# One ordering edge and the order of the last two column blocks in a two-layer encoder

## The chip, the cores and the metric

The kernel runs on one core of one Trainium2 chip. The metric is the device time of one execution in microseconds (us). The kernel before takes 2002.78 us (median of three runs, 2001.56 to 2003.46).

A core has five engines, each with its own queue of instructions that it works off in order. TensorE (PE) multiplies; its weight loads (PEld) overlap the multiplications. VectorE (DVE), ScalarE (ACT) and GpSimd (POOL) do element-wise work, and SyncE (SP) issues DMA transfers. Engines wait for each other by semaphores.

## The reference

The reference is a trunk of two encoder layers over 256 tokens of width 2048, in float32. Each layer has attention (layer 0: neighbourhood attention; layer 1: grouped-query attention; both beside four cross-attention heads into 256 memory tokens), an output projection, and an MLP. What concerns this change is the MLP and the end:

```python
n = rms_norm(h, mlp_norm[i])
h = h + jnp.square(jax.nn.relu(n @ w_up[i])) @ w_down[i]
...
return rms_norm(h, final_norm)
```

`w_up` is 2048 x 8192 and `w_down` 8192 x 2048. The final norm divides each token's row by its root mean square and multiplies by `final_norm` column by column.

## The kernel before

The 256 tokens lie in two token tiles of 128 partitions (`NT` = 2). Every float32 matrix product is made of three products of rounded numbers: each operand is split into a high part (a copy on ScalarE, L507) and a low part (the original minus the high part, on VectorE, L508), and TensorE adds high x high, high x low and low x high. So every weight that comes from HBM passes through ScalarE and VectorE before TensorE can use it.

**The up projection** makes 128 hidden columns at a time (`up_grains`, number m of 64), as two grains of eight k-steps each. After it, `squared` applies ReLU and square; when m is odd, the two columns m-1 and m make a *pair* (number m // 2), for which VectorE forms sums and differences of its four 128x128 blocks (L1122 to L1124) and splits them into `a_s` (L1126). That split is what `box["made"]` remembers.

**The down projection** takes 30 of the 32 pairs for each half of the output columns by a Strassen scheme with seven products in place of eight (`down_grains`, step n of 60; `STEPS` gives the half q and the pair j of each step; steps 0 and 1 are pairs 0 and 1 of half 1, step 2 is pair 0 of half 0). One step loads a 1 MB chunk `b` of four 128x512 blocks and needs besides three running sums of them:

- `lift`: ScalarE copies block 3 into `t` (L1165), and an accumulating DMA of GpSimd adds block 1 to it (L1166).
- `pre`: VectorE forms the three other sums of `t`, one on top of the other (L1172 to L1174).
- `prep_first` splits `b` into `bh`, `bl`; `prep_second` splits `t` into `th`, `tl`. These four rooms exist once each.
- `run`: TensorE's first half has three products (nine matmuls with `bh`, `bl`), its second half four (twelve matmuls with `th`, `tl`; L1195, L1198, L1199).

The grains of a layer's MLP stand in a list: four up projections, and then for each step the first half of the down step, the two grains of an up projection, and the second half. While grain k runs, loads, sums and splits of grains some places ahead are traced; `pre` is traced five grains ahead, the splits four.

**Order on an engine.** The order in which the instructions of one engine stand in its queue is worked out by a planner when the program is built: it simulates the program in time and takes what is ready, earlier-traced work first. The kernel adds edges: `tc.issue_after(x)` says that the instructions in its block stand behind instruction x in the queue of x's engine. No semaphore is added by it. In `pre`, steps 1 and 2 have such an edge behind the split that `box["made"]` holds at that moment; it is the split of the latest pair traced by then. `pin` keeps marked instructions in the order in which the program lists them.

**The end.** The two pairs that are left over are summed plainly, by column blocks of 512 in the order 2, 0, 1, 3 (`REST`; `plain_grains`). A block has two pieces of weights, of two k-steps each; both token tiles are summed together, piece by piece, in `m_products` (L388, L391, L392). Then `down_done` adds the sums to `h` (L1241), takes the squares on ScalarE (L920), and for layer 1 multiplies by `final_norm` (L1358). In layer 1 the last block (3) is different: it is summed tile by tile, tile 0 in one part of 512 columns and tile 1 in two parts of 256, and each part goes to `finish`. It adds to `h` (L1409), forms the mean of squares over all four blocks, takes its power -1/2 on GpSimd (L1432), multiplies the tile's row (L1433 to L1435 on VectorE and ScalarE), and issues three DMA transfers to the output (L1438).

Of the kernel before, what the change touches and what calls it, by code (L numbers as in the profile page):

```python
# [14 lines left out]
ALU = mybir.AluOpType  # L15
# [144 lines left out]
def encoder_kernel(ctx: ExitStack, tc: tile.TileContext, t: dict, out: bass.AP):  # L160
# [945 lines left out]
    def squared(layer, m, ps):  # L1106

        e = m % 2
        if e == 0:
            box["c"] = at.mlp.tile([P, 8, P], F32, tag="c", bufs=2, name="c")  # L1110
        c = box["c"]
        two = c[:, 2 * e : 2 * e + 2, :].rearrange("p a b -> p (a b)")
        box["relu"] = nc.scalar.activation(two, ps, AF.Relu)
        nc.scalar.activation(two, two, AF.Square)
        if e == 0:
            return
        pair = m // 2
        if pair >= max(STEPPED):
            a = at.mlp.tile([P, 2, 4, P], F32R, tag="a", bufs=6, name="a_p")
            split(a[:, 0], a[:, 1], c[:, :4])  # L1120
        else:
            nc.vector.tensor_tensor(c[:, 4, :], c[:, 0, :], c[:, 2, :], op=ALU.subtract)  # L1122
            nc.vector.tensor_tensor(c[:, 5:7, :], c[:, 0:8:4, :], c[:, None, 1, :].to_broadcast([P, 2, P]), op=ALU.add)
            nc.vector.tensor_tensor(c[:, 7, :], c[:, 3, :], c[:, 6, :], op=ALU.subtract)  # L1124
            a = at.mlp.tile([P, 2, 7, P], F32R, tag="a", bufs=6, name="a_s")
            box["made"] = split(a[:, 0], a[:, 1], c[:, 1:])[1]  # L1126
            if pair >= min(STEPPED):

                n = pair - min(STEPPED)
                if n == 0:  # L1130
                    box["a_0"] = at.mlp.tile([P, max(STEPPED) - min(STEPPED), 2, P], F32R, tag="a", bufs=6, name="a_0")
                split(box["a_0"][:, n, 0], box["a_0"][:, n, 1], c[:, 0])
        box["a", pair] = a
        if m == UPS - 1 and layer == 1:
            later(2, load_gf)
# [11 lines left out]
    def down_grains(layer, n, begins, ends, sooner):  # L1147

        q, j = STEPS[n]
        own = {}  # L1150

        def load():
            own["b"] = at.side.tile([P, 4, 512], F32, tag="b", bufs=3, name="b")
            nc.sync.dma_start(own["b"].rearrange("p a b -> p (a b)"),
                              t[f"w_pair{layer}"][j * 2 + q])

        def behind(fn, far=4):

            return (lambda: past(fn, box["splits"][-far])) if n < 2 else fn

        def lift():

            b, s = own["b"], at.side.tile([P, 4, 512], F32, tag="T", bufs=2, name="t")
            own["t"] = s
            nc.scalar.activation(s[:, 3, :], b[:, 3, :], AF.Copy)  # L1165
            nc.gpsimd.dma_start(s[:, 3, :], b[:, 1, :], accum_op=ALU.add)  # L1166

        def pre():

            b, s = own["b"], own["t"]  # L1170
            with tc.issue_after(box["made"].ins) if n in (1, 2) else nullcontext():
                nc.vector.tensor_tensor(s[:, 0, :], b[:, 3, :], b[:, 0, :], op=ALU.add)  # L1172
            nc.vector.tensor_tensor(s[:, 1, :], s[:, 0, :], b[:, 1, :], op=ALU.add)
            nc.vector.tensor_tensor(s[:, 2, :], s[:, 1, :], b[:, 2, :], op=ALU.add)  # L1174

        def prep_first():
            own["first"] = tuple(at.mlp.tile([P, 3 * 512], F32R, tag=x, name=x) for x in ("bh", "bl"))
            split(*own["first"], own["b"].rearrange("p a b -> p (a b)")[:, : 3 * 512])

        def prep_second():  # L1180
            own["second"] = tuple(at.mlp.tile([P, CH], F32R, tag=x, name=x) for x in ("th", "tl"))
            with tc.issue_after(box["relu"].ins) if n == 0 else nullcontext():
                split(*own["second"], own["t"].rearrange("p a b -> p (a b)"))

        def run(which, products):
            if n == 0 and which == "first":
                open_strassen(layer)
            hi, lo = own.pop(which)
            a = box["a", j]
            for name, ai, bi in products:  # L1190
                if n == 0:
                    sum_of(name)
                entered = begins and not (name in SHARED and q in box["z_set"])
                ps, s = box["ps"][name], slice(bi * 512, (bi + 1) * 512)
                ins = nc.tensor.matmul(ps, a[:, 0, ai, :], hi[:, s], start=entered, stop=False,  # L1195
                                       skip_group_check=True)
                pin(ins)
                nc.tensor.matmul(ps, a[:, 0, ai, :], lo[:, s], start=False, stop=False, skip_group_check=True)  # L1198
                nc.tensor.matmul(ps, a[:, 1, ai, :], hi[:, s], start=False, stop=ends, skip_group_check=True)  # L1199

        def after(products):
            if ends:
                for name, _, _ in products:
                    taken(q, name)
                    if n + 1 < len(STEPS):
                        seeded(STEPS[n + 1][0], name)

        def after_second():
            after(SECOND)
            if ends:  # L1210
                box["z_set"].add(q)
            if ends and j == STEPPED[q] - 1:
                folded(q, 0.5 if n == len(STEPS) - 1 else 1)

        return [Grain(lambda: run("first", FIRST), lambda: after(FIRST), load, behind(pre), behind(prep_first, 4 if n else 1),
                      (8 if n < 2 else 12, 8 if sooner else 5, 4), behind(lift)),
                Grain(lambda: run("second", SECOND), after_second, None, None, behind(prep_second), SOONER)]
# [62 lines left out]
    def plain_grains(layer, nb, at_chunk):  # L1280

        last = layer == 1 and nb == REST[-1]
        w = Work("M", None, left_of, 0, True, True, None, finish if last else down_done(layer, nb))
        nc_ = len(chunks_left(nb))
        own = {}

        def load(c):
            own[c] = loaded(t[f"w_plain{layer}"][at_chunk + c], "Ub"[(at_chunk + c) % 2])

        def prep(c, hf):  # L1290
            if (at_chunk + c) % 2 == 0:
                own[c, hf] = half_of_side(own[c], hf, MOVING_AT)
            else:
                own[c, hf] = tuple(at.mlp.tile([P, HALF], F32R, tag="bt"[hf] + x, name=f"{x}_p") for x in "hl")
                box["rest"] = split(*own[c, hf], own[c][:, hf * HALF : (hf + 1) * HALF])


        PIECES = [(c, hf, ((UPS // 2 - min(STEPPED)) // 2 - nc_ + c) * 4 + hf * 2, 2) for c in range(nc_) for hf in range(2)]

        def begin():  # L1300
            if nb == REST[0]:
                closed("ps_sums")
                open_sums(layer)
            w.ps = [at.acc.tile([P, 512], F32, tag="acc", name="ps_m") for _ in range(NT)]
            if last:

                w.ps.append(at.acc.tile([P, 512], F32, tag="acc", name="ps_m"))

        def run(n):
            if last:  # L1310
                return
            c, hf, k0, nk = PIECES[n]
            if n == 0:
                begin()
            for i in range(NT):
                m_products(w, k0, nk, i, *own[c, hf], n == 0, n == len(PIECES) - 1)

        def after():
            if not last:
                w.done(w)  # L1320
                return

            begin()

            for i, bank, part in ((0, 0, (0, 512)), (1, 1, (0, 256)), (1, 2, (256, 512))):
                for n, (c, hf, k0, nk) in enumerate(PIECES):
                    m_products(w, k0, nk, i, *own[c, hf], n == 0, n == len(PIECES) - 1, keep_order=True, part=part,
                               bank=bank)
                w.done(w, i, bank, *part)

        return [Grain(lambda n=n: run(n), after if n == len(PIECES) - 1 else None,
                      (lambda c=c: load(c)) if hf == 0 else None, None, lambda c=c, hf=hf: prep(c, hf), SOON)
                for n, (c, hf, _, _) in enumerate(PIECES)]
# [21 lines left out]
    def times_gf(nb):  # L1355
        s = slice(nb * 512, (nb + 1) * 512)
        for i in range(NT):
            nc.vector.tensor_tensor(h[:, i, s], h[:, i, s], box["gf"][:, s], op=ALU.mult)  # L1358

    def down_done(layer, nb):  # L1360
        def f(w):
# [419 lines left out]
```

## Time and profile before

| | before |
|---|---|
| time, median of three runs | 2002.78 us |
| profiled execution: time | 2002.76 us |
| profiled execution: span, first to last instruction | 2001.0 us |
| mean granted TensorE clock | 0.997 of full |
| TensorE busy | 1984.8 us, 99% |
| VectorE busy | 1726.2 us, 86% |
| ScalarE busy | 1443.1 us, 72% |
| HBM read | 397.78 MB |

All starts of instructions are counted from the start of the span. A row of a timeline has the start, the duration, the engine, the line of the program, the operation with its output and inputs by the program's names, the shape, and how many were merged into the row (x2); in brackets stands how long the engine had been idle and which instruction released it. Row durations of one engine overlap a little at their ends, so the next start says more of the pace than the sum of durations. `c`, `t`, `b`, `th`, `tl`, `bh`, `bl`, `uh`, `ul`, `a_s` are the rooms named above (`uh`, `ul` are the split weights of the up projection); `first` in the rows of the end is the tile that holds `h`.

### The profile page before, as it was taken

What the parts mean: (1) busy time and instruction counts of PE and PEld (TensorE: products, weight loads), DVE (VectorE), ACT (ScalarE), POOL (GpSimd) and SP (SyncE); (2) the same over time, 40 slices, a digit from 0 to 9 for tenths busy, and PEclk for the clock granted to TensorE, in tenths of its full rate; (3) what the DMA queues carried; (4) which work ended last, traced back from release to release, by engine and by line L of the source; (5) the groups of instructions that cost most, each with busy time, mean ns of one, the idle gap of its engine ahead of it and who ended that gap; (6) DMA issues with size and microseconds to landing.
All of it is one profiled execution on the core that took longest, in us unless ns stands there. A gap on an engine that the chain in (4) does not pass through costs nothing.

```text
span 2001.0 us, 33096 instructions
## 1 busy us (share of the span) xinstructions
PE 1984.8 (99%) x12832; PEld 1801.8 (90%) x12832; DVE 1726.2 (86%) x2096; ACT 1443.1 (72%) x2105; POOL 149.9 (7%) x205
## 2 busy tenths in 40 slices
PE   9999999999999999999999999999999999999998
PEld 9999999898999999999998888898999999999997
DVE  6777767579999999999999869778999999999997
ACT  6655555577887788877887666667788777877786
POOL 0000000000000000000001011000000000000001
PEclk9999999999999999999999999999999999999999
DMA  7855555667777777777778765667777777777775
GB/s 288 320 193 204 206 192 185 261 211 217 223 228 237 234 235 235 221 241 226 229 227 229 263 216 174 225 202 229 226 226 230 237 231 231 237 226 243 228 225 152
DMA packets 110685, 452.46 MB, mean 226 GB/s; under 512 B 18880, under 2 KB 40640, under 8 KB 63168
## 3 DMA queue, kind: packets, MB, share of 16 engines
q1 hardware_dynamic: 90144, 413.38, 60.3%
q0 software_dynamic: 20096, 36.45, 10.4%
q8 instruction: 100, 1.64, 0.3%
q14 instruction: 57, 0.47, 0.1%
q10 hardware_dynamic: 288, 0.52, 0.1%
HBM read 397.78 MB, written 4.19 MB: 201 GB/s over the span
## 4 chain that ended last, share of the span: by engine, by line
PE 98%; DVE 1%; ACT 1%; issue 0%; POOL 0%; DVEq 0%; POOLq 0%
PE ps_u L411 35%; PE p L1198 10%; PE p L1199 10%; PE p L1195 10%; PE ps_s L411 9%; PE ps_m L391 8%; PE ps_m L392 8%; PE ps_m L388 7%; PE sc_ps L604 0%; PE sc_ps L605 0%; PE sc_ps L603 0%; PE av L696 0%; PE av L697 0%; PE av L698 0%; PE idle L240 0%
## 5 line engine op out<-in xcount | busy, mean ns | idle before, releaser
L411 PE MATMUL ps_u<-hT,uh 128*128 128x256 f32 x3874 | 674.5, 276 | 0.0
L411 PEld LDWEIGHTS ps_u<-hT,uh 128*128 128x128 f32 x3874 | 588.5, 188 | 5.8
L411 PE MATMUL ps_u<-hT,ul 128*128 128x256 f32 x1994 | 550.7, 276 | 0.0
L507 ACT ACTIVATE uh<-raw_U 128x1024 fp32r<-128x1024 f32 x262 | 277.5, 1060 | 154.3 <-PE ps_u L411 149.8
L411 PEld LDWEIGHTS ps_u<-hT,ul 128*128 128x128 f32 x1994 | 374.3, 188 | 0.0
L507 ACT ACTIVATE hi<-raw 128x1024 fp32r<-128x1024 f32 (+1 forms) x215 | 222.0, 1037 | 183.0 <-PE ps_m L392 94.2
L508 DVE TENSOR_TENSOR lo<-raw,hi 128x1024 fp32r<-128x1024 f32 (+1 forms) x215 | 255.0, 1190 | 108.4 <-ACT hi L507 107.7
L508 DVE TENSOR_TENSOR ul<-raw_U,uh 128x1024 fp32r<-128x1024 f32 x262 | 319.6, 1220 | 15.7 <-ACT uh L507 15.7
L508 DVE TENSOR_TENSOR tl<-t,th 128x2048 fp32r<-128x2048 f32 x120 | 274.7, 2290 | 57.5 <-ACT th L507 57.3
L507 ACT ACTIVATE th<-t 128x2048 fp32r<-128x2048 f32 x120 | 230.8, 1924 | 90.4 <-PE p L1199 90.4
L508 DVE TENSOR_TENSOR bl<-b,bh 128x1536 fp32r<-128x1536 f32 x120 | 210.3, 1752 | 0.3 <-ACT bh L507 0.3
L1198 PE MATMUL p<-tl,a_s 128*128 128x512 f32 x480 | 188.9, 394 | 5.7 <-DVE tl L508 5.7
L1166 POOL DMA_DIRECT2D t<-b x120 | 104.2, 869 | 1169.4 <-ACT t L1165 1113.2
L1195 PE MATMUL p<-th,a_s 128*128 128x512 f32 x480 | 188.8, 393 | 0.2
L1199 PE MATMUL p<-th,a_s 128*128 128x512 f32 x480 | 188.0, 392 | 0.0
L507 ACT ACTIVATE bh<-b 128x1536 fp32r<-128x1536 f32 x120 | 178.6, 1488 | 3.7
L411 PE MATMUL ps_s<-nT,hi 128*128 128x256 f32 x896 | 154.6, 277 | 0.0
L1199 PE MATMUL p<-bh,a_s 128*128 128x512 f32 x360 | 140.9, 391 | 0.0
L1198 PE MATMUL p<-bl,a_s 128*128 128x512 f32 x360 | 140.1, 389 | 0.0
L1195 PE MATMUL p<-bh,a_s 128*128 128x512 f32 x360 | 140.1, 389 | 0.0
L411 PEld LDWEIGHTS ps_s<-nT,hi 128*128 128x128 f32 x896 | 135.3, 188 | 0.2
L411 PE MATMUL ps_s<-nT,lo 128*128 128x256 f32 x448 | 124.2, 277 | 0.0
(292 smaller groups left out, 3639.9 us busy)
## 6 DMA issues: line engine op xcount, KB each, us to landing
raw_U<-in_w_up SPq DMA_DIRECT2D x128, 1024.0 KB, 6.3
b<-in_w_pair SPq DMA_DIRECT2D x120, 1024.0 KB, 5.8
raw<-in_w_o SPq DMA_DIRECT2D x32, 1024.0 KB, 5.0
t<-b POOLq DMA_DIRECT2D x120, 256.0 KB, 6.5
raw<-in_w_b SPq DMA_DIRECT2D x21, 1024.0 KB, 5.7
raw<-in_w_av SPq DMA_DIRECT2D x12, 1024.0 KB, 5.0
raw<-in_w_aq SPq DMA_DIRECT2D x12, 1024.0 KB, 5.0
raw<-in_w_ak SPq DMA_DIRECT2D x12, 1024.0 KB, 4.9
```

The costliest lines, as they stand in the source:

```text
L388: first = nc.tensor.matmul(ps, ah, hi[:, s], start=st, stop=False)
L391: nc.tensor.matmul(ps, ah, lo[:, s], start=False, stop=False)
L392: final = nc.tensor.matmul(ps, al, hi[:, s], start=False, stop=sp)
L411: ins = nc.tensor.matmul(ps, x, acts[:, k, part], start=k == n == 0, stop=k == KT - 1 and n == 2)
L507: first = nc.scalar.activation(dst_hi, src, AF.Copy)
L508: return first, nc.vector.tensor_tensor(dst_lo, src, dst_hi.bitcast(F32), op=ALU.subtract)
L1166: nc.gpsimd.dma_start(s[:, 3, :], b[:, 1, :], accum_op=ALU.add)
L1195: ins = nc.tensor.matmul(ps, a[:, 0, ai, :], hi[:, s], start=entered, stop=False, skip_group_check=True)
L1198: nc.tensor.matmul(ps, a[:, 0, ai, :], lo[:, s], start=False, stop=False, skip_group_check=True)
L1199: nc.tensor.matmul(ps, a[:, 1, ai, :], hi[:, s], start=False, stop=ends, skip_group_check=True)
```

## The change

The split of a pair is remembered under the pair's number, and the sums of step n (n = 1 or 2) stand behind the split of pair n - 1, where both stood behind the latest split traced. This is done in both layers.

In layer 1 the last two column blocks, 1 and 3, are interleaved by token tile: block 1's grains sum token tile 0 alone, and what is done with the result is done for that tile; then block 3's tile 0 is summed and finished; then block 1's tile 1 is summed with its own additions, squares and multiplication; then block 3's tile 1 follows in its two parts as before.

```diff
-            box["made"] = split(a[:, 0], a[:, 1], c[:, 1:])[1]
+            box["made", pair] = split(a[:, 0], a[:, 1], c[:, 1:])[1]
...
-            with tc.issue_after(box["made"].ins) if n in (1, 2) else nullcontext():
+            with tc.issue_after(box["made", n - 1].ins) if n in (1, 2) else nullcontext():
                 nc.vector.tensor_tensor(s[:, 0, :], b[:, 3, :], b[:, 0, :], op=ALU.add)
...
+        parted = layer == 1 and nb == REST[-2]
...
-            for i in range(NT):
+            for i in range(1 if parted else NT):
                 m_products(w, k0, nk, i, *own[c, hf], n == 0, n == len(PIECES) - 1)
 
+        def second():
+            for n, (c, hf, k0, nk) in enumerate(PIECES):
+                m_products(w, k0, nk, 1, *own[c, hf], n == 0, n == len(PIECES) - 1, keep_order=True)
+            tile_done(w, nb, 1)
+
         def after():
+            if parted:
+                tile_done(w, nb, 0)
+                box["second"] = second
+                return
...
             for i, bank, part in ((0, 0, (0, 512)), (1, 1, (0, 256)), (1, 2, (256, 512))):
+                if bank == 1:
+                    box["second"]()
                 for n, (c, hf, k0, nk) in enumerate(PIECES):
...
+    def tile_done(w, nb, i):
+        s = slice(nb * 512, (nb + 1) * 512)
+        add_scaled(h[:, i, s], w.ps[i], box["inv"][:, i : i + 1])
+        sum_squares(3, i, nb)
+        nc.vector.tensor_tensor(h[:, i, s], h[:, i, s], box["gf"][:, s], op=ALU.mult)
```

## The prediction

> **What bounds the kernel now.** I read the page first, then TensorE's own waits.
>
> ```profile
> span 2001.0 us, 33096 instructions
> PE 1984.8 (99%) x12832; PEld 1801.8 (90%) x12832; DVE 1726.2 (86%) x2096; ACT 1443.1 (72%) x2105; POOL 149.9 (7%) x205
> PE p L1198 <- DVE tl L508: 5.7, 2, 2.8
> ```
>
> The reader is to see that TensorE is the bound: time can come only from its idle time, from matmuls at a lower clock, or from what follows its last matmul. The third line (the waits of TensorE) says that apart from the kernel's first microsecond it waited twice, 5.7 us together, both times for a VectorE instruction that writes `tl`, the low part of a step's sums. The timeline of TensorE puts one in each layer, in the second half of step 1 of the stepped down projection (layer 0, then an undisturbed step 2, then layer 1; start, duration):
>
> ```profile
> 460.48 0.50 PE L1195 MATMUL p<-th,a_s 128*128 128x512 f32 x1
> 463.82 0.50 PE L1198 MATMUL p<-tl,a_s 128*128 128x512 f32 x1 [2.84 <-DVE tl L508]
> 468.02 0.39 PE L1195 MATMUL p<-bh,a_s 128*128 128x512 f32 x1
> 475.52 0.40 PE L1195 MATMUL p<-th,a_s 128*128 128x512 f32 x1
> 478.25 0.39 PE L1195 MATMUL p<-bh,a_s 128*128 128x512 f32 x1
> 1369.01 0.50 PE L1195 MATMUL p<-th,a_s 128*128 128x512 f32 x1
> 1372.35 0.76 PE L1198 MATMUL p<-tl,a_s 128*128 128x512 f32 x1 [2.84 <-DVE tl L508]
> 1376.58 0.39 PE L1195 MATMUL p<-bh,a_s 128*128 128x512 f32 x1
> ```
>
> The twelve matmuls of such a half take 478.25 - 475.52 = 2.73 us in step 2, but 468.02 - 460.48 = 7.54 us in step 1 of layer 0 and 1376.58 - 1369.01 = 7.57 us in layer 1. So a stall costs 4.81 and 4.84 us, not its 2.84 us of idle time. The rest, about 1.97 us, is clock. Busy time by stretches (stretch, length, TensorE busy, granted clock, DMA share, GB/s):
>
> ```profile
> 464.50:467.50 3.00, 3.00 (x9) 0.50 0.60 131
> 1372.30:1375.70 3.40, 3.35 (x8) 0.52 0.72 198
> ```
>
> After each stall some 3.4 us of matmuls ran at half clock.
>
> Why `tl` is late stands in VectorE's timeline of layer 0 (rows in between are left out; the last one is of layer 1):
>
> ```profile
> 440.38 1.09 DVE L508 TENSOR_TENSOR a_s<-c,a_s 128x896 fp32r<-128x896 f32 x1 [1.02 <-ACT a_s L507]
> 443.39 1.23 DVE L508 TENSOR_TENSOR ul<-raw_U,uh 128x1024 fp32r<-128x1024 f32 x1 [0.79 <-ACT uh L507]
> 445.47 2.29 DVE L508 TENSOR_TENSOR tl<-t,th 128x2048 fp32r<-128x2048 f32 x1 [0.85 <-ACT th L507]
> 451.49 1.07 DVE L508 TENSOR_TENSOR a_s<-c,a_s 128x896 fp32r<-128x896 f32 x1
> 452.48 1.29 DVE L1172 TENSOR_TENSOR t<-b 128x512 f32<-128x512 f32 x2
> 457.48 1.28 DVE L1174 TENSOR_TENSOR t<-t,b 128x512 f32<-128x512 f32 x2
> 458.68 1.75 DVE L508 TENSOR_TENSOR bl<-b,bh 128x1536 fp32r<-128x1536 f32 x1
> 461.49 2.28 DVE L508 TENSOR_TENSOR tl<-t,th 128x2048 fp32r<-128x2048 f32 x1
> 470.66 2.29 DVE L508 TENSOR_TENSOR tl<-t,th 128x2048 fp32r<-128x2048 f32 x1 [1.55 <-ACT th L507]
> ...
> 1361.00 1.29 DVE L1172 TENSOR_TENSOR t<-b 128x512 f32<-128x512 f32 x2
> ```
>
> The first sum (L1172) of step 1 and of step 2 come as a pair, x2, directly behind pair 1's split (`a_s` at 451.49): both wait for the same split. The sums are not done before 458, and `tl` starts at 461.49, when TensorE already wants it. VectorE has no gap in this time (a stretch; busy time of TensorE, its loads, VectorE third with 5.00 of 5.00, ScalarE, GpSimd):
>
> ```profile
> 455.00:460.00 5.00, 5.00 (x47) 5.00 (x46) 5.00 (x8) 4.08 (x4) 0.00 (x0) 1.00 0.78 241
> ```
>
> Layer 1 has the same picture 908.5 us later.
>
> **Part one: the edge of step 1.** When step 1's sums are traced, the latest pair that was split is pair 1; when step 2's are traced it still is pair 1. So the new key changes step 1 alone, from pair 1 to pair 0; step 2 keeps its wait. No instruction is added or removed. Three sums of about 0.64 us each (half of the 1.29 us of 452.48), 1.9 us in all, may now stand behind pair 0's split, from 441.4 on. Their data are there, by ScalarE's timeline:
>
> ```profile
> 437.30 0.63 ACT L1165 ACTIVATE t<-b 128x512 f32<-128x512 f32 x1 [0.70 <-DMA b<-in_w_pair]
> 454.27 0.60 ACT L1250 ACTIVATE z<-p 128x512 f32<-128x512 f32 x1 [1.32 <-PE p L1199]
> 458.53 1.90 ACT L507 ACTIVATE th<-t 128x2048 fp32r<-128x2048 f32 x1
> ```
>
> Step 1's chunk `b` had landed by 437.30, where ScalarE copies from it; no DMA is moved by the edge itself. VectorE idles 0.79 and 0.85 us before its instructions of 443.39 and 445.47, 1.64 us that take in most of the 1.9; the other 0.3 us is pushed on to what follows. I cost the move at nothing, since the 0.3 is covered too: what is pushed to the end of the full stretch is pair 1's split, which ends at 452.56, and the first half of step 1 wants it here:
>
> ```profile
> 452.71 0.39 PE L1195 MATMUL p<-bh,a_s 128*128 128x512 f32 x1
> 453.16 0.39 PE L1199 MATMUL p<-bh,a_s 128*128 128x512 f32 x1
> ```
>
> L1199 reads the low part, 0.60 us after the split's end. If the planner puts all three sums behind 445.47 that cover is gone, and TensorE idles 1.9 - 0.6 = 1.3 us more in each layer. Between 0 and 1.3 I take 0.
>
> **Where `tl` goes then.** The room `th` is free when the last matmul of step 0's second half has read it, at about 452.8 (the row of 452.71 follows it). ScalarE is idle for the 1.32 us up to 454.27, so `th` can run from 452.8 for 1.9 us, and `tl` from 454.7 to 457.1. TensorE wants it at 460.48 + 0.23 = 460.7. At the other end, all other work keeps its order: `th` stays at 458.53, ends at 460.43, `tl` runs 460.45 to 462.7, and the idle time falls only from 2.84 to 1.8 us. I take the early end, no stall, because the row of 470.66 shows how the order comes out in a step whose sums are done: VectorE itself waits for `th` there, with nothing put ahead of `tl`. What is late next would be `bl` of step 2 (458.68): TensorE then reaches its row of 468.02 at 463.2. `bl` ended at 460.43; it loses 1.9 us of sums ahead of it, gains 2.3 us of `tl` and up to 1 us of waiting for `th`, and ends near 461.8, 1.4 us early. So each layer gives back 4.81 and 4.84 us.
>
> The Trainium skill ("TensorE: Matmul & The Clock Gate", Part 1) puts the fall to half clock at an idle window of about 3.4 us; this trace has it after 2.84 us of idle time. By that window alone removing the stalls would give 2 x 2.84 us; by the rows it is 9.65.
>
> **Part two: the last two column blocks.** The same matmuls, squares, adds and multiplications are issued; block 1's second token tile (12 matmuls, 2.73 us) moves behind block 3's first. The end of TensorE does not move. The rows of the end before:
>
> ```profile
> 1986.05 0.39 PE L388 MATMUL ps_m<-h_p,a_p 128*128 128x512 f32 x1
> 1991.52 0.28 PE L392 MATMUL ps_m<-h_p,a_p 128*128 128x256 f32 x1
> 1982.29 1.22 DVE L508 TENSOR_TENSOR l_p<-raw_b,h_p 128x1024 fp32r<-128x1024 f32 x1
> 1986.25 0.75 DVE L1241 SCALAR_TENSOR_TENSOR first<-ps_m,inv,first 128x512 f32<-128x512 f32 x1 [0.38 <-PE ps_m L392]
> 1986.92 0.68 DVE L1358 TENSOR_TENSOR first<-first,gf 128x512 f32<-128x512 f32 x1
> 1988.97 0.75 DVE L1409 SCALAR_TENSOR_TENSOR first<-ps_m,inv,first 128x512 f32<-128x512 f32 x1 [0.36 <-PE ps_m L392]
> 1990.40 0.48 DVE L1409 SCALAR_TENSOR_TENSOR first<-ps_m,inv,first 128x256 f32<-128x256 f32 x1 [0.68 <-PE ps_m L392]
> 1991.92 0.75 DVE L1433 SCALAR_TENSOR_TENSOR first<-first,fin_r,gf 128x512 f32<-128x512 f32 x1
> 1992.59 0.75 DVE L1435 TENSOR_SCALAR first<-first,fin_r 128x1024 f32<-128x1024 f32 x1
> 1993.25 0.48 DVE L1409 SCALAR_TENSOR_TENSOR first<-ps_m,inv,first 128x256 f32<-128x256 f32 x1
> ```
>
> The last matmul ends at 1991.80, yet its add starts at 1993.25: tile 0's two final multiplications, 1.33 us, stand ahead of it. With tile 0 done 2.73 us earlier they can start near 1989.0, and the last add at 1991.84, a gain of 1.41 us at most. But block 1's second add and multiplication (0.67 + 0.60 us) now come after 1988.97 too. From there VectorE has those, the two multiplications (1.33), the add of 1990.40 (0.48) and the small work that stood between its end at 1990.88 and 1991.92: of that 1.04 us I count 0.6 as busy, an estimate. That is 3.7 us without a gap: the last add at 1992.7, a gain of 0.6, and with the other 0.4 us as waits 0.2. I take 0.9 us, nearer to the 1.41, since the planner may put block 1's multiplication behind the last add. Block 3's weights, whose low part ends at 1983.51, are now wanted by its second piece at 1986.05 - 2.73 + 1.36 = 1984.7; that covers it by 1.2 us.
>
> **The sum**, against the profiled execution's 2002.76 us (its span of 2001.0 and 1.76 around it; the median of the runs, 2002.78, is the same): 2002.76 - 4.81 - 4.84 - 0.9 = 1992.2 us.
>
> **Rivals.** (1) The stalls are only shortened: the early-order argument fails, `th` stays behind other work of ScalarE, 1.8 us of idle time remain. Saved per layer 1.0 us if the clock still falls, 3.0 us if it doesn't: with the end's 0.9, 1999.8 or 1995.8 us. For it speaks that `th` was put behind another split at 458.53; against it the 1.32 us gap. No row has an idle time of 1.8 us; by the skill's window the second holds. (2) The edge moves nothing in the planner's order, or the stall turns up again at step 2, whose first half comes 4.8 us sooner: VectorE's queue has no gap from 445.47 to past 461.49, which speaks for it, the 1.4 us of margin against it. Only the end's gain is left, 2001.9. (3) Slower: the freed `tl` is placed ahead of pair 1's split in VectorE's fixed order. It must wait for `th`, to 454.7, then takes 2.29 us and the split 1.07: L1199 of 453.16 waits until 458.0, 4.9 us, and half clock follows, 1.97. Each layer loses 6.8 and saves 4.8: 2002.76 + 4.0 - 0.9 = 2005.9. It decides once the split ends after 453.16 + 4.8 - 1.97 = 456.0. Against it: pair 1's split comes first in program order, and was ready at 451.5, before `th` could be.
>
> **Chances.** Forecast 0.66, shortened 0.14 (half for each time), no effect or moved 0.14, slower 0.06. About 0.2%, 4 us, is what a measurement of this kernel tells from no change, so below 1998.8 is faster: 0.66 + 0.07, rounded to 0.74; slower by more than that 0.05; the rest 0.21. The likeliest case's own range is 1991.0 to 1994.5 (all gains full: 1991.7). With the shortened stalls the range is 1990.8 to 2000.2.
>
> **What would show it.** Right: no wait of TensorE for `tl`; full clock in every stretch of both layers; step 1's three sums between 441 and 446, only one L1172 behind 452.5; the last L1409 no more than 1.2 us after the last matmul's end, where it was 1.45. Wrong: a wait in step 1 or step 2 with another releaser (`bl`, `a_s`, `th`), half clock after it, or L1433 of tile 0 still ahead of the last add.

## The result, and the profile after

| | before | after |
|---|---|---|
| time, median of four runs | 2003.02 us (2001.56 to 2003.46) | 1991.27 us (1990.38 to 1992.31) |
| profiled execution: time, span | 2002.76, 2001.0 us | 1992.31, 1990.5 us |
| TensorE busy | 1984.8 us | 1980.6 us |
| mean granted clock | 0.997 | 0.999 |
| last matmul's end to the span's end | 9.20 us | 8.49 us |

The ratio to the kernel before is 0.9943, with a 95% interval of 0.9926 to 0.996. A second measurement, five runs, gave 1991.43 us and 0.9944 (0.9932 to 0.9957). The kernel is 0.6% faster.

The page of the kernel after, and the only wait of TensorE for another engine above 0.2 us:

```profile
span 1990.5 us, 33096 instructions
PE 1980.6 (100%) x12832; PEld 1799.3 (90%) x12832; DVE 1725.6 (87%) x2096; ACT 1442.2 (72%) x2105; POOL 149.9 (8%) x205
PE idle L240 <- POOL mhalf L234: 1.0, 1, 1.0
```

The waits for `tl` are gone from both layers; what stays is the kernel's first microsecond. The second half of step 1 by TensorE's timeline, layer 0 and then layer 1:

```profile
460.61 0.40 PE L1195 MATMUL p<-th,a_s 128*128 128x512 f32 x1
460.84 0.39 PE L1198 MATMUL p<-tl,a_s 128*128 128x512 f32 x1
463.34 0.39 PE L1195 MATMUL p<-bh,a_s 128*128 128x512 f32 x1
1364.06 0.40 PE L1195 MATMUL p<-th,a_s 128*128 128x512 f32 x1
1366.79 0.39 PE L1195 MATMUL p<-bh,a_s 128*128 128x512 f32 x1
```

The twelve matmuls take 463.34 - 460.61 = 2.73 us in layer 0 and 2.73 us in layer 1, where they took 7.54 and 7.57: no idle time, no slow clock. Why stands in VectorE's timeline of the kernel after (layer 0, the last two rows layer 1; rows in between are left out):

```profile
440.50 1.09 DVE L508 TENSOR_TENSOR a_s<-c,a_s 128x896 fp32r<-128x896 f32 x1 [1.02 <-ACT a_s L507]
441.51 0.69 DVE L1172 TENSOR_TENSOR t<-b 128x512 f32<-128x512 f32 x1
442.23 0.69 DVE L1173 TENSOR_TENSOR t<-t,b 128x512 f32<-128x512 f32 x1
443.97 0.69 DVE L1174 TENSOR_TENSOR t<-t,b 128x512 f32<-128x512 f32 x1
446.10 2.29 DVE L508 TENSOR_TENSOR tl<-t,th 128x2048 fp32r<-128x2048 f32 x1 [0.30 <-ACT th L507]
452.12 1.07 DVE L508 TENSOR_TENSOR a_s<-c,a_s 128x896 fp32r<-128x896 f32 x1
453.11 0.68 DVE L1172 TENSOR_TENSOR t<-b 128x512 f32<-128x512 f32 x1
457.50 2.29 DVE L508 TENSOR_TENSOR tl<-t,th 128x2048 fp32r<-128x2048 f32 x1
459.70 1.75 DVE L508 TENSOR_TENSOR bl<-b,bh 128x1536 fp32r<-128x1536 f32 x1
...
1344.51 0.69 DVE L1172 TENSOR_TENSOR t<-b 128x512 f32<-128x512 f32 x1
1360.73 2.29 DVE L508 TENSOR_TENSOR tl<-t,th 128x2048 fp32r<-128x2048 f32 x1
```

Step 1's three sums now run at 441.51, 442.23 and 443.97, directly behind pair 0's split, and only one L1172 (step 2's) is left behind pair 1's split at 452.12. `th` follows them forward on ScalarE:

```profile
453.48 1.90 ACT L507 ACTIVATE th<-t 128x2048 fp32r<-128x2048 f32 x1
```

It stood at 458.53 before. `tl` ends at 459.79, 1.05 us ahead of the matmul of 460.84 that reads it.

The end of the kernel after, TensorE's last matmul and VectorE's rows around it (small ones are left out):

```profile
1981.73 0.28 PE L392 MATMUL ps_m<-h_p,a_p 128*128 128x256 f32 x1
1979.85 0.74 DVE L1451 SCALAR_TENSOR_TENSOR first<-first,fin_r,gf 128x512 f32<-128x512 f32 x1
1980.51 0.75 DVE L1453 TENSOR_SCALAR first<-first,fin_r 128x1024 f32<-128x1024 f32 x1
1981.17 0.48 DVE L1427 SCALAR_TENSOR_TENSOR first<-ps_m,inv,first 128x256 f32<-128x256 f32 x1
1982.23 0.47 DVE L1427 SCALAR_TENSOR_TENSOR first<-ps_m,inv,first 128x256 f32<-128x256 f32 x1
1982.62 0.41 DVE L1447 TENSOR_TENSOR first<-first,gf 128x256 f32<-128x256 f32 x1
1983.33 0.48 DVE L1433 CUSTOM_DVE_ANT_0 sq_t<-first,fin_v 128x256 f32<-128x256 f32 x1
```

(The lines of the end are 18 higher than before: L1427 was L1409.) Tile 0's two multiplications, 1979.85 and 1980.51, are done before the last matmul ends at 1982.01, and the last add starts 0.22 us behind it, where it was 1.45. But the last square (L1433) starts 1.32 us behind it, where it was 1993.76 - 1991.80 = 1.96: it gained 0.64, not 1.23. From the last add to the last square VectorE works without a gap: the add, the multiplication of tile 1's first part (L1447) and the small sums of the mean. Before, that multiplication and the small sums stood ahead of the last add. So the last square starts 1983.33 - 1982.23 = 1.10 us behind the add, where it was 1993.76 - 1993.25 = 0.51.

### The profile page after: what moved, and what is told of

Read it like the earlier page. It is cut to its first block, busy times and chain, and to the rows that moved or that the text cites. A ratio compares the mean times of both kernels' runs of the same rounds, so it can differ in the third digit from the quotient of the medians.

```text
span 1990.5 us, 33096 instructions
## 1 busy us (share of the span) xinstructions
PE 1980.6 (100%) x12832; PEld 1799.3 (90%) x12832; DVE 1725.6 (87%) x2096; ACT 1442.2 (72%) x2105; POOL 149.9 (8%) x205
## 4 chain that ended last, share of the span: by engine, by line
PE 97%; ACT 1%; DVE 1%; DMA 1%; issue 0%; DVEq 0%; SPq 0%; POOLq 0%; POOL 0%; ACTq 0%
PE ps_u L411 35%; PE p L1195 10%; PE p L1199 10%; PE p L1198 10%; PE ps_s L411 9%; PE ps_m L391 7%; PE ps_m L392 7%; PE ps_m L388 7%; DMA first<-in_x 0%; ACT sq L856 0%; PE sc_ps L604 0%; PE sc_ps L605 0%; PE sc_ps L603 0%; PE av L696 0%; PE av L697 0%
```

## The experiments

My theory: the edge alone removes both stalls, the interleaved blocks shorten the end by less than a microsecond, and the two do not touch each other. The rivals: the end carries part of the gain; the stalls hang together through the planner or come from something else than the sums; an idle time of the order of 1 to 3 us has another price than the one in the sum.

**The edge alone.**

```diff
-            box["made"] = split(a[:, 0], a[:, 1], c[:, 1:])[1]
+            box["made", pair] = split(a[:, 0], a[:, 1], c[:, 1:])[1]
...
-            with tc.issue_after(box["made"].ins) if n in (1, 2) else nullcontext():
+            with tc.issue_after(box["made", n - 1].ins) if n in (1, 2) else nullcontext():
```

> The edge alone, with the end of the kernel as before. My theory: all but the end's part of the gain comes from step 1's sums standing behind pair 0's split in VectorE's queue, 4.81 and 4.84 us in the two layers and some 0.3 us more in each, since the weight load of step 1's second half no longer waits for th either: 2002.8 - 10.2 = 1992.6 us, no wait of TensorE for tl, and the stretch from the last matmul's end to the span's end stays at 9.2 us as before. Rival (the end carries part of what I gave to the stalls): 1995 us or more.

Measured: 1991.69 us (1990.97 to 1992.31), ratio 0.9943 (0.9929 to 0.9958), against 2003.38 us for the kernel before on the same chip. No wait for `tl`. The last matmul ends at 1981.37 in a span of 1990.5, so the end is 9.13 us, as before. The edge alone is the measured gain; the rival falls.

**The last two blocks alone**: the changed kernel with the two lines above put back.

> The interleaved last two blocks alone, with both sums behind the latest split as before. My theory: both waits of 2.84 us for tl and the half clock behind them stay, and only the end is shorter, by 0.7 us (last matmul's end to the span's end 8.5 us in place of 9.2): 2002.1 us, not to be told from before by its time. Rival (the end is worth more than its own rows): under 2000 us.

Measured: 2002.27 us (2001.04 to 2003.35), ratio 0.9994 (0.9985 to 1.0004). By the time no difference can be told. TensorE's rows of layer 0:

```profile
460.63 0.50 PE L1195 MATMUL p<-th,a_s 128*128 128x512 f32 x1
463.96 0.50 PE L1198 MATMUL p<-tl,a_s 128*128 128x512 f32 x1 [2.83 <-DVE tl L508]
467.67 0.63 PE L1195 MATMUL p<-bh,a_s 128*128 128x512 f32 x1
```

The stall stands as before; the last matmul ends at 1992.22 in a span of 2000.8, an end of 8.58 us. So the interleaving is worth 0.6 to 0.7 us in the trace, which the time cannot confirm.

**The edge in layer 0 only.** (`pre` takes pair 0's split in layer 0 and the latest one in layer 1.)

```diff
-            with tc.issue_after(box["made"].ins) if n in (1, 2) else nullcontext():
+            with tc.issue_after((box["made"] if layer else box["made", n - 1]).ins) if n in (1, 2) else nullcontext():
```

> The edge moved in layer 0 only, the end as before. My theory: the stalls are independent, each the work of its own layer's edge; layer 0 loses its wait and 5.1 us, layer 1 keeps a wait of 2.8 us for tl in step 1 with half clock behind it: 1997.7 us. Rival (the layers' orders hang together in the planner, or the stall comes from the state of the loads): layer 1's wait changes by more than 0.5 us too, or layer 0's stays.

Measured: 1998.93 us in one run. Layer 0 has no wait; layer 1 has it:

```profile
1364.01 0.49 PE L1195 MATMUL p<-th,a_s 128*128 128x512 f32 x1
1367.35 0.80 PE L1198 MATMUL p<-tl,a_s 128*128 128x512 f32 x1 [2.85 <-DVE tl L508]
1372.21 0.63 PE L1195 MATMUL p<-bh,a_s 128*128 128x512 f32 x1
```

The stalls are independent, as I held. The time misses 1997.7 by 1.2 us, and the rows say where: with the same 2.85 us of idle time these twelve matmuls took 8.20 us, not 7.57, and the nine behind them 1374.58 - 1372.21 = 2.37 us from the first start to the last, where 1.81 is usual. Half clock lasted longer here. Its rows (stretch, length, TensorE busy, granted clock, DMA share, GB/s; cut where the clock changes):

```profile
1363.09:1366.50 3.41, 1.29 (x9) 1.00 0.86 353
1366.50:1369.91 3.41, 2.56 (x6) 0.50 0.70 240
1369.91:1373.33 3.42, 3.42 (x9) 0.50 0.92 269
```

The stall of 2.85 us, up to 1367.35, lies across the edge at 1366.50. Half clock began while TensorE still waited and held for two such windows, 6.83 us, where the kernel before has one, 3.41 us.

**No edge for step 1 at all**, in the changed kernel: is the place behind pair 0 needed, or only freedom from pair 1?

```diff
-            with tc.issue_after(box["made", n - 1].ins) if n in (1, 2) else nullcontext():
+            with tc.issue_after(box["made", n - 1].ins) if n == 2 else nullcontext():
```

> The changed kernel without any edge for step 1's sums (step 2 keeps its edge). The sums then stand ahead of bl of step 0 and of pair 0's split in VectorE's queue and push these back by up to 1.9 us. My theory: what matters is that the sums are done before pair 1's split; step 0's first half has some 1 to 1.5 us of cover for pair 0's split, so TensorE waits between 0 and 0.8 us there in each layer: 1991.3 to 1993 us. Rival (the edge behind pair 0 is what protects step 0): a wait of 1 us or more for a_s in step 0 of each layer, with half clock behind it, 1995 us or more.

Measured: 1992.37 us in one run. TensorE's rows of step 0's first half, layer 0:

```profile
442.06 0.50 PE L1195 MATMUL p<-bh,a_s 128*128 128x512 f32 x1
443.18 0.50 PE L1199 MATMUL p<-bh,a_s 128*128 128x512 f32 x1 [0.40 <-DVE a_s L508]
443.52 0.39 PE L1195 MATMUL p<-bh,a_s 128*128 128x512 f32 x1
```

The sums stood around `bl` of step 0 and between the sums of pair 0, whose split (`a_s`) started only at 442.04: the first three matmuls take 443.52 - 442.06 = 1.46 us, and 1.00 us in layer 1, where the changed kernel takes 0.70 and 0.71. No half clock follows. So freedom from pair 1 is nine tenths of the gain, and the place behind pair 0 keeps about 1 us.

**`tl` late by choice.** The chances of the prediction had two prices for a shortened stall, with half clock behind it and without. To measure it, the changed kernel forms the first columns of step 1's `tl` twice. What is computed stays the same; the planner puts `bl` of step 2 between the two, so `tl` is late by an amount that the number of columns sets.

```diff
-                split(*own["second"], own["t"].rearrange("p a b -> p (a b)"))
+                box["late_tl"] = split_late(nc, *own["second"], own["t"].rearrange("p a b -> p (a b)"), ((512,), (1024,))[layer] if n == 1 else ())
...
+def split_late(nc, hi, lo, src, again):
+    nc.scalar.activation(hi, src, AF.Copy)
+    for n in (*again, CH):
+        last = nc.vector.tensor_tensor(lo[:, :n], src[:, :n], hi[:, :n].bitcast(F32), op=ALU.subtract)
+    return last
```

> The changed kernel with VectorE forming a part of step 1's tl twice (512 columns more in layer 0, 1024 in layer 1), which puts bl of step 2 between the two and makes tl late by choice. tl should end near 462.0 us in layer 0 and, for 1024 columns, about 1.4 us too late in layer 1: TensorE idles some 1.0 and 1.4 us. It measures the price that was disputed for a shortened stall. If the clock halves only after an idle window of about 3.4 us, or if it needs the 2.84 us of the kernel before, the twelve matmuls of step 1's second half take 2.73 us plus the idle time and nothing more (3.8 and 4.1 us). If any idle time of that order halves the clock, they take up to 2 us more (5.5 to 6 us).

> The same with 1536 columns formed twice in both layers: TensorE idles some 2.2 us in layer 0 and 2.0 us in layer 1. With full clock the twelve matmuls take 4.9 and 4.7 us; with half clock for 3.4 us behind it 6.9 and 6.7 us. The page's window of about 3.4 us says full clock; the kernel before, half clock after 2.84 us, leaves both open.

> As the two runs with tl late by choice: 1024 columns formed twice in layer 0, 1280 in layer 1, for some 1.7 us of idle time in both, between the 1.41 us that left the clock alone and the 1.95 us that halved it. If there is one threshold of idle time, both layers come out alike. If it is a window that runs on its own, in which the idle time must take a certain share, the two may differ, since they lie at other places in it. A half with full clock loses about 2.0 us, one with half clock about 3.7 us.

TensorE's rows in the first of the three (layer 0, then layer 1's wait; L1804 is the line of the new function):

```profile
459.44 0.40 PE L1195 MATMUL p<-th,a_s 128*128 128x512 f32 x1
460.81 0.50 PE L1198 MATMUL p<-tl,a_s 128*128 128x512 f32 x1 [0.98 <-DVE tl L1804]
463.44 0.39 PE L1195 MATMUL p<-bh,a_s 128*128 128x512 f32 x1
...
1365.95 0.50 PE L1198 MATMUL p<-tl,a_s 128*128 128x512 f32 x1 [1.41 <-DVE tl L1804]
```

in the second (1536 columns in both layers; the last two rows are the clock's window with layer 1's stall and the one behind it):

```profile
459.90 0.40 PE L1195 MATMUL p<-th,a_s 128*128 128x512 f32 x1
462.66 0.80 PE L1198 MATMUL p<-tl,a_s 128*128 128x512 f32 x1 [2.36 <-DVE tl L1804]
466.74 0.39 PE L1195 MATMUL p<-bh,a_s 128*128 128x512 f32 x1
1369.81 0.50 PE L1198 MATMUL p<-tl,a_s 128*128 128x512 f32 x1 [1.95 <-DVE tl L1804]
...
1366.93:1370.34 3.41, 1.46 (x10) 1.00 0.52 168
1370.34:1373.75 3.41, 3.41 (x9) 0.50 0.89 238
```

and in the third (1024 and 1280 columns; the last three rows are the clock's window with layer 0's stall, and the clock in a longer stretch around it and in layer 1):

```profile
462.49 0.50 PE L1198 MATMUL p<-tl,a_s 128*128 128x512 f32 x1 [1.66 <-DVE tl L1804]
1367.92 0.50 PE L1198 MATMUL p<-tl,a_s 128*128 128x512 f32 x1 [1.69 <-DVE tl L1804]
...
459.69:463.10 3.41, 1.75 (x12) 1.00 0.56 168
460.00:468.00 8.00, 6.34 (x35) 1.00 0.80 236
1365.00:1375.00 10.00, 8.31 (x52) 1.00 0.77 232
```

All eleven halves, two of them in the kernel before, beside each other; "lost" is the time of the twelve matmuls less 2.73 us. The clock is granted in windows of 3.41 us (last section); the second column is the idle time in the window that has most of it:

| idle time before `tl`'s matmul | most in one window | the twelve matmuls | lost | clock behind it |
|---|---|---|---|---|
| 0.98 | 0.98 | 4.00 | 1.27 | full |
| 1.41 | 1.06 | 4.44 | 1.71 | full |
| 1.66 | 1.66 | 4.69 | 1.96 | full |
| 1.69 | 1.40 | 4.72 | 1.99 | full |
| 1.95 | 1.95 | 6.56 | 3.83 | half |
| 2.36 | 2.09 | 6.84 | 4.11 | half |
| 2.83 to 2.85 (five halves) | 2.04 to 2.84 | 7.04 to 8.20 | 4.31 to 5.47 | half |

Up to 1.69 us a stall costs itself and 0.3 us; from 1.95 us on, another 1.2 to 2.3 us within the half. In two of the five long stalls the half clock ran on into the nine matmuls behind (2.35 and 2.37 us, usually 1.81), so that the cost within the half is not all of it. In one run each the three kernels took 1994.11, 1999.58 and 1996.08 us: the second, with 4.3 us of idle time in both layers together, lost 7.9 us in its halves, and the third, with 3.4 us, 4.0.

**The end once more.** Tile 0's last multiplication on ScalarE, to free the add that the mean hangs on; and then block 1's multiplication for tile 1 behind the last square too.

```diff
-        nc.vector.tensor_scalar(h[:, i, 512:x], h[:, i, 512:x], r, None, op0=ALU.mult)
+        if i:
+            nc.vector.tensor_scalar(h[:, i, 512:x], h[:, i, 512:x], r, None, op0=ALU.mult)
+        else:
+            nc.scalar.activation(h[:, i, 512:x], h[:, i, 512:x], AF.Copy, scale=r)
```

> The changed kernel with token tile 0's last multiplication of 1024 columns on ScalarE in place of VectorE. In the changed kernel the add of tile 1's first part starts at 1981.17, 0.6 us after its matmuls' end, because that multiplication stands ahead of it, and the mean that the last square needs hangs on this add. My theory: the mean comes 0.6 us sooner, and the stretch from the last matmul's end to the span's end goes from 8.5 to 7.9 us: 1990.7 us by the median. Rival (the end is bound by the output's transfers, 1 MB for each tile): the stretch stays at 8.5 us.

Measured: 1991.22 us in its one run; the end is 1989.4 - 1981.07 = 8.33 us, 0.16 less than the changed kernel's and not 0.6. The mean's add did start 0.6 us sooner, but the last square came only 0.17 us sooner, 1.15 us after the last matmul. I put that down to block 1's multiplication for tile 1, which stood ahead of the last add. So the second edit:

```diff
+        if i == 0:
             nc.vector.tensor_tensor(h[:, i, s], h[:, i, s], box["gf"][:, s], op=ALU.mult)
...
-            nc.vector.tensor_tensor_reduce(sq, hs, hs, 1.0 / D, box["mean"], ALU.mult, ALU.add, m)
+            last = nc.vector.tensor_tensor_reduce(sq, hs, hs, 1.0 / D, box["mean"], ALU.mult, ALU.add, m)
+            b = slice(REST[-2] * 512, (REST[-2] + 1) * 512)
+            with tc.issue_after(last.ins):
+                nc.vector.tensor_tensor(h[:, i, b], h[:, i, b], box["gf"][:, b], op=ALU.mult)
```

> The changed kernel with token tile 0's last multiplication of 1024 columns on ScalarE, and with block 1's multiplication for tile 1 behind the last square in VectorE's queue, into the 0.67 us in which VectorE waits for GpSimd's power. In the run with the first of the two alone, that multiplication (0.60 us) stood ahead of the last add's small work, and the last square started 1.15 us after the matmuls' end. My theory: it now starts 0.6 us after it, and the stretch from the last matmul's end to the span's end falls from 8.33 to 7.8 us; by time 0.6 us under the changed kernel, too little to be sure of. Rival (the output's transfers set the end): the stretch stays within 0.2 us of 8.33.

> The changed kernel once more, beside the run with the end's work moved. 1991.3 us, ratio to before 0.9943; the stretch from the last matmul's end to the span's end 8.5 us.

Measured: 1991.4 us (1991.23 to 1992.12) with both edits and 1991.43 us (1990.92 to 1991.77) for the changed kernel on the same chip; the ends are 8.56 and 8.55 us. Nothing is gained. The last square starts 1.02 us after the last matmul's end, sooner than in any other of these kernels, but not the 0.6 that I expected. The reason given there was wrong. With the first edit the last add already started 0.04 us after the last matmul's end (1981.11 and 1981.07), and the last square 1.11 us behind the add; with both edits it is 0.03 us and 0.99 us. What sets the square is VectorE's own work behind the last add, and the last add cannot start before its matmuls end. Then the power of the mean on GpSimd, which comes next, took longer. GpSimd's row in the kernel with the first edit alone:

```profile
1982.79 0.55 POOL L1450 TENSOR_TENSOR fin_r<-fin_v,mhalf 128x1 f32<-128x1 f32 x1 [4.82 <-DVE fin_v L1433]
```

and with both, beside the multiplication of VectorE that was put there:

```profile
1983.33 0.94 POOL L1454 TENSOR_TENSOR fin_r<-fin_v,mhalf 128x1 f32<-128x1 f32 x1 [4.69 <-DVE fin_v L1434]
1983.17 0.69 DVE L1437 TENSOR_TENSOR first<-first,gf 128x512 f32<-128x512 f32 x1
```

The gap that I meant to fill wasn't free. The rival, that the output's transfers set the end, does not hold either: from the end of VectorE's last instruction to the span's end it is 4.7 to 4.8 us in the kernel before, in the changed one, with the first edit and with both, so the transfers follow this chain. No version here beats the changed kernel by more than its noise.

## Why the prediction was right

Measured were 1991.27 us where 1992.2 was predicted; by the profiled executions 10.45 us less where 10.55 was. By the medians the gain is 11.75 us here and 10.86 in the second measurement; runs of one kernel differ by about 2 us, so the terms are read from the profile. Term by term:

- **The two stalls, predicted 4.81 and 4.84 us.** Both went whole; the edge alone and the end alone show that the edge did it. The term was 0.27 us too small in each layer: it began at 460.48, the first matmul of the half, and left out that this matmul's weights had themselves waited for `th`. Of the 1.97 us that it put down to clock, 0.3 is lost at full clock too, as the late `tl` shows. The row of the missing term was there, among the waits of the weight loads before:

```profile
PEld p L1195 <- ACT th L507: 0.6, 2, 0.3
```

From the last matmul of step 1's first half to the first of its second, 454.52 to 460.48 took 5.96 us before, and 454.92 to 460.61 takes 5.69 now. Together 10.2 us: from the start of step 0's second half (449.96 before, 450.38 after) to the last matmul (1991.52 and 1981.73) the difference is 1541.56 - 1531.35 = 10.21.
- **The move at no cost.** Right in the profiled execution, but not in every one. Here VectorE's gaps took the sums in whole and nothing was pushed on: `tl` of step 0 still waits 0.30 us for `th`. Pair 1's split ends at 453.19, 0.37 us ahead of its matmul of 453.56, where it had been 0.60; the 0.23 us is what TensorE gained on the way (10.27 us from step 0's first half to step 1's, 10.50 before). That cover was the thinnest one. In other executions `tl` of step 0 did not wait, since the sums pushed it on, and in three of them the cover was gone in layer 0: at a price of 0.15 us in the second measurement of the changed kernel, and of some 0.3 us in the kernel with both edits at the end and in the second one with a late `tl`. The row of the first:

```profile
452.86 0.50 PE L1199 MATMUL p<-bh,a_s 128*128 128x512 f32 x1
```

- **Where `tl` goes.** Right in the end, wrong in the reason. I took the early end because of a later step in which nothing stood ahead of `tl`. Here step 2's sums, a `ul` and two adds stood ahead of it, and it came at 457.50, not 454.7. The margin was 1.05 us and not the 3.6 us that the row of 470.66 had suggested. `bl` of step 2, which I named as the next one late, ended at 461.45 (461.8 expected), 1.9 us early.
- **The end, predicted 0.9 us, 0.71 measured** in the profile. The last add moved by 1.23 us, near the top of the bounds; the step that failed is the assumption that the end follows this add. It follows the last square, and of VectorE's work ahead of that square 0.6 us more now stands behind the last add (1.10 us from the add's start to the square's, 0.51 before).
- The remainder: this profiled execution reached step 0 in layer 0 0.63 us later than the one before (442.84 and 442.21), ahead of all that was changed, and its second half still 0.42 us later (450.38 and 449.96). That, the 0.55 us of `th` and the 0.2 us of the end nearly cancel, which is luck.

The rivals: a shortened stall did not come, but it was nearer than its 0.14 suggests, since 1.05 us of delay would have brought it. Its two prices are now known: with 1.8 us of idle time it would have stood between them, in the range from 1.66 to 1.95 us that no run covers. (The chance of a faster kernel adds up to 0.73 there, not 0.74.) The slower rival, `tl` ahead of pair 1's split, was not seen in any order.

## What to carry to other kernels

Where a stall shows half clock behind it, cost it by the time of the group of instructions against an undisturbed group, not by the idle time: here 2.84 us of idle time were 5.1 us with the clock and the weights' wait. An edge that holds work back should name the event that the work is to be kept behind, not the latest one traced: two steps had met behind the same split, and an engine with idle time 10 us earlier was the bottleneck later. In the last microseconds, follow the value that is needed last through all the work that its engine still has ahead of it; an add made early is worth little when that work only moves behind the add.

## What the runs showed of the hardware

**TensorE's clock was granted in fixed windows of 3.41 us, and a little over half a window of idle time halved it.** Behind all seven stalls that lost the clock, half clock lasted 3.41 us, or twice that in the one case where 0.85 us of the first window was idle too (1366.50 to 1373.33, the edge in layer 0 only). Three kernels have two such stalls each, 907.15 to 908.79 us apart; yet in all three 904.53 us lie between the end of the first half clock and the start of the second, 265 times 3.413 us. So the windows run on their own, and a stall counts by what falls into one window. The clock fell behind windows with 1.95 to 2.84 us of idle time and stayed full behind those with up to 1.66 us; the stall of 1.69 us had only 1.40 us in one window. This also explains why 2.83 to 2.85 us of idle time lost anything from 4.31 to 5.47 us in the half: the stalls lay differently to the edges. With one sample at each length, a sharp threshold between 1.66 and 1.95 us is not shown.

The Trainium skill ("TensorE: Matmul & The Clock Gate", Part 1) gives an idle window of about 3.4 us for the fall, full clock after about 3.4 us of sustained work, and a window that runs on its own. The last two agree with the rows here; the first does not agree, and the measurement decides: a little over half of that window was enough.

**GpSimd took longer beside a VectorE multiplication with two inputs in SBUF.** The one-column power took 0.55 to 0.57 us in the other 23 rows of the twelve traces, and 0.94 us in the one in which such a multiplication of 0.69 us had started 0.16 us ahead of it. That the multiplication is the cause is inferred from this one row. The Trainium skill ("SBUF — State Buffer", "SBUF: two separate sides") says that a VectorE instruction with two SBUF inputs and a GpSimd instruction that reads SBUF exclude each other on a shared pair of ports; the row agrees, though it shows one case only.
